# A third landing buffer for the feed-forward weight stream of a diffusion layer, in memory taken from two small tiles

## The chip, the cores and the metric

The kernel runs on one core of a Trainium2 chip. The metric is the device time of one execution in microseconds, and lower is better. The engines are named as the profile names them: PE is the matrix engine (PEld is its weight load), DVE the vector engine, ACT the scalar engine, POOL the GpSimd engine, SP the engine that issues most of the DMAs.

## The reference

One layer of a hybrid backbone on 128 context tokens and 256 latent tokens (384 in all, width 2048, float32). The parts that matter here:

```python
def layer(x, cond, s0_f, s0_b, n_chunks, lw):
    mod = jax.nn.silu(cond) @ lw['w_ada'] + lw['b_ada']
    sh1, sc1, ga1, sh2, sc2, ga2 = [m[:, None, :] for m in jnp.split(mod, N_MOD, axis=-1)]
    h = rmsnorm(x, lw['norm_pre_mix']) * (1.0 + sc1) + sh1
    m, s_f, s_b = mixer(h, s0_f, s0_b, n_chunks, lw)
    x = x + ga1 * rmsnorm(m, lw['norm_post_mix'])
    h = rmsnorm(x, lw['norm_pre_ffn']) * (1.0 + sc2) + sh2
    ff = (jax.nn.silu(h @ lw['w_ffn_gate']) * (h @ lw['w_ffn_up'])) @ lw['w_ffn_down']
    x = x + ga2 * rmsnorm(ff, lw['norm_post_ffn'])
    return x, s_f, s_b
```

`mixer` is a gated linear attention and a Fourier branch, whose inside the change does not touch. The feed-forward has 5632 hidden channels: gate and up weights of 2048 x 5632, down weights of 5632 x 2048. `cond` has two columns, one for context and one for latent tokens, and `mod` has six parts of 2048 channels each.

## The kernel before

**Stages.** The program runs in one pass: the first norm with the first two modulation parts and the first products (to 146 us in the profile below), the other input projections beside the attention, the Fourier branch and the merge (to about 740 us), the output projection (to 893 us), the second norm, and from about 910 us the feed-forward to the end. Weights come from memory in blocks of 128 x 1024 floats (512 KB).

**A weight block's way.** Each float32 matmul is done as three products of rounded parts. A block lands in a tile called `raw` (or `u`, `dw`, see below), ACT casts it to `whi` (lines 225 and 1431), DVE subtracts to get the remainder `wlo` (lines 226 and 1442), and PE takes both. `whi` and `wlo` have four buffers each, `raw` has two in the pool `wp`. The instructions of PE, ACT, DVE and POOL stand in the order in which the code records them; only those of SP are placed by a scheduler, and SP runs them in that order.

**The feed-forward.** The hidden width is cut into 11 chunks. Each chunk computes gate and up products in the steps A, B, C, E, F, G, H (`pgu`, with sums of blocks that save products, Strassen's way), and the down products of the chunk before are set between these steps (`pds`, `pdn`). Five kinds of step read a streamed block through `raw` (`STREAM`: C, G, D, DC, DG); the steps A, B, DA, DB read blocks that are kept in ten resident slots (`u`, `dw`) over several steps. Before each step, `grab2` takes the split block, issues further loads (`load_more`, line 1396) and splits the next one (`split_next`, line 1421). `load_more` keeps at most two streamed blocks loaded and not yet split (`out_now[0] < 2`), then up to two resident loads. Since there are two `raw` buffers, the load of a block waits on SP for the remainder of the block two before it (DVE, line 1442).

**Other work in the feed-forward.** DVE makes the sixth modulation part from small blocks `w<-in_w_ada` (line 1470 loads, line 1475 multiplies and adds; `ada_last`). Finished down products are added up in memory (`sums_d`): ACT copies them out, POOL issues an adding DMA (line 1667), and SP loads them back in the last chunk (`back` and `psums`, lines 1677 and 1693). Hidden blocks are turned by DMA from ACT's queue (line 1610), two per chunk, and ACT takes the result at line 1616 before it copies the sums of step A out (line 1574).

**The two small tiles.** `spad` holds silu of the conditioning, padded from 2 to 32 columns (2 KB a partition); PE reads it in the first stage as a stationary operand, and DVE reads its two real columns for parts three to six, to the end of the kernel. `adev` (1 KB a partition) takes the modulation sums `pr` out of PSUM before PE turns them (lines 585 and 1490). In the output projection the tile of the modulation sums `adacc` serves as two more landing buffers (`raw2`, line 1106).

Of the kernel before, what the change touches and what calls it, by code (L numbers as in the profile page):

```python
# [11 lines left out]
F32 = mybir.dt.float32  # L12
# [4 lines left out]
ALU = mybir.AluOpType  # L17
# [4 lines left out]
P = 128  # L22
D = 2048
KT = D // P
# [13 lines left out]
G = 1024  # L38
# [59 lines left out]
def tile_step(ctx: ExitStack, tc: tile.TileContext, a, o):  # L98
    nc = tc.nc
    PE, ACT, DVE, POOL, SP = nc.tensor, nc.scalar, nc.vector, nc.gpsimd, nc.sync  # L100
    ctx.enter_context(nc.allow_non_contiguous_dma(reason="small column loads"))

    const = ctx.enter_context(tc.tile_pool(name="const", bufs=1))
    actp = ctx.enter_context(tc.tile_pool(name="actp", bufs=1))
    wp = ctx.enter_context(tc.tile_pool(name="wp", bufs=4))
    dram = ctx.enter_context(tc.tile_pool(name="dram", bufs=1, space=DRAM))

    cond = const.tile([P, KT, 2], F32, name="cond")
    SP.dma_start(cond, a["cond"])
    spad = const.tile([P, KT, 32], F32, name="spad")  # L110
    POOL.memset(spad, 0.0)
    eps_t = const.tile([P, 1], F32, name="eps_t")
    ones = const.tile([P, P], F32, name="ones")
    POOL.memset(eps_t, EPS)
# [42 lines left out]
    for i in range(8):  # L157
        k = (0, 1, 1, 2, 1, 2, 1, 2)[i]
# [136 lines left out]
                    start=n == 0, stop=n == len(src) - 1,  # L295
                )

    def warm(dst, n):

        for _ in range(n):  # L300
            PE.matmul(dst, ones, spad.rearrange("p a b -> p (a b)")[:, 0:T], start=True, stop=True)
# [15 lines left out]
    pss = ctx.enter_context(tc.tile_pool(name="pss", bufs=5, space=PSUM))  # L317
    with ExitStack() as s:
        pa = s.enter_context(tc.tile_pool(name="pa", bufs=1))
        pb = s.enter_context(tc.tile_pool(name="pb", bufs=2))  # L320
        slabs = {}

# [53 lines left out]
        px = pss.tile([P, T], F32, tag="side", name="px")  # L376
# [51 lines left out]
            return mm, lambda dst=None: flush(lracc, kb == 0, dst)  # L428

        ACT.activation(spad[:, :, 0:2], cond, AF.Silu)  # L430
        ACT.activation(tmp1, eps_t, AF.Sqrt)
        qs = [pa.tile([P, T], F32, name=f"qsA{n}") for n in range(2)]
        for k in range(KT):
            sq = qs[k] if k < 2 else scr[:, 4 + k % 4, :]
            ACT.activation(sq, xn(k), AF.Square)
            if k >= 2:
                DVE.tensor_add(qs[k % 2], qs[k % 2], sq)
        warm(px, 11)

        for t in range(3):  # L440
            for n, q in enumerate(qs):
# [10 lines left out]
        ev = pb.tile([P, 256], F32, tag="ev", name="ev")  # L452
# [6 lines left out]
        for kb in range(KT):  # L459
# [31 lines left out]
            if kb:  # L491
                ev = pb.tile([P, 256], F32, tag="ev", name="ev")
# [10 lines left out]
            if kb == 0:  # L503
# [6 lines left out]
                op0=ALU.add, op1=ALU.mult,  # L510
            )
            DVE.tensor_scalar_add(mods[:, 0, kb, :], pm[:, 0:2], cols[:, 0, kb : kb + 1])
            for lo, hi, c in segs:
                DVE.tensor_scalar(
                    hf[:, lo:hi], xr[:, lo:hi], mods[:, 1, kb, c : c + 1], mods[:, 0, kb, c : c + 1],
                    op0=ALU.mult, op1=ALU.add,
# [43 lines left out]
    adap = ctx.enter_context(tc.tile_pool(name="adap", bufs=1))  # L560

    def ada_rest(todo):
        for m in todo:
            for half in range(2):
                acc = adap.tile([P, 2, 1024], F32, tag="adacc", name="adacc")
                for k in range(KT):
                    w = adap.tile([P, 1024], F32, tag="adaw", name="adaw", bufs=2)
                    SP.dma_start(w, a["w_ada"][m - 2, half, k])
                    for c in range(2):
                        if k == 0:  # L570
                            DVE.tensor_scalar_mul(acc[:, c, :], w, spad[:, k, c : c + 1])
                        else:
                            DVE.scalar_tensor_tensor(  # L573
                                acc[:, c, :], w, spad[:, k, c : c + 1], acc[:, c, :], op0=ALU.mult, op1=ALU.add,
                            )
                    yield
                yield
                pr = pss.tile([P, 256], F32, tag="side", name="pr")
                for c in range(2):
                    for j in range(4):  # L580
                        PE.matmul(
                            pr[32 * j : 32 * j + 32, :], selr[:, 32 * c : 32 * c + 32],
                            acc[:, c, j * 256 : (j + 1) * 256], start=c == 0, stop=c == 1,
                        )
                ev = adap.tile([P, 256], F32, tag="adev", name="adev")
                ACT.copy(ev, pr)
                yield
                pt = pss.tile([P, 2, P], F32, tag="side", name="ptm")
                for b in range(2):
                    PE.transpose(pt[:, b, :], ev[:, b * P : (b + 1) * P], ident)  # L590

                src = pt.rearrange("p b (j r) -> p j b r", r=32)
                mh = mods[:, m, 8 * half : 8 * half + 8, :]
                for c in range(2):
                    DVE.tensor_copy(mh[:, :, c].rearrange("p (j b) -> p j b", b=2), src[:, :, :, c])
                bc = lambda v: v[:, 8 * half : 8 * half + 8].unsqueeze(2).to_broadcast([P, 8, 2])
                DVE.tensor_add(mh, mh, bc(bsc1[:, 1, :] if m == 4 else cols[:, m, :]))
                w1 = {2: 1, 4: 2, 5: 3}.get(m)
                if w1 is not None:
                    DVE.tensor_mul(mh, mh, bc(norms[:, w1, :]))  # L600
# [12 lines left out]
    with ExitStack() as s:  # L613
# [203 lines left out]
        for c in range(2):  # L817

            dst = a2.rearrange("p (h d j) -> p d h j", d=2, j=P)[:, c]
            raw, up = (x.rearrange("p (h j) -> p h j", j=P) for x in (raw3[1 + c][0:98, 0:512], part[0:98]))  # L820
# [28 lines left out]
    with ExitStack() as s:  # L849
# [11 lines left out]
        pairs = [x[:, n * pw : n * pw + 2 * HT] for x, k in ((cl, 6), (d2, 2)) for n in range(k)]  # L861
# [184 lines left out]
    with ExitStack() as s:  # L1046
# [49 lines left out]
        for i in range(KT):  # L1096
            p = psm.tile([P, T], F32, tag="mm", name="pmm")
            for g in range(2):
                n = 2 * i + g - 2 * KT
                if n < -6:  # L1100
                    w = grab()
                else:

                    w = take()
# [162 lines left out]
        pf = s.enter_context(tc.tile_pool(name="pf", bufs=1))  # L1267
# [103 lines left out]
        pairs = []  # L1371
# [3 lines left out]
        for kind, c, i in steps:  # L1375
            e = [kind, c, i, None]
# [4 lines left out]
        for c in range(1, NFC):  # L1381
            resident += [(kind, c, i) for kind in "AB" for i in range(4)]
            if c < LAST:
                resident += [("DA", c - 1, 0), ("DB", c - 1, 0)]
        out_now = [sum(e[3] is not None for e in entries)]
        free = set(range(10))

        def slot(x, kind, c, i):
# [5 lines left out]
            return t.rearrange("p (i x) -> p i x", i=2 if kind[0] == "D" else FC)  # L1394

        def load_more(kept=1):
            while pairs and out_now[0] < 2:
                e, src = pairs.pop(0)
                e[3] = wp.tile([P, G], F32, tag="raw", name="raw", bufs=2)
                SP.dma_start(e[3] if e[0] == "R" else fold_of(e[0], e[3]), src)  # L1400
                out_now[0] += 1
            while kept and resident:
                kind, c, i = resident[0]
                k = slot(kind[-1] == "B", kind, c, i)
                if k not in free or k >= len(slots):
                    return
                free.remove(k)
                SP.dma_start(fold_of(kind, slots[k]), src_of(kind, c, i))
                resident.pop(0)
                kept -= 1  # L1410
# [53 lines left out]
        def ada_last():  # L1464
            m = 5
            acc, wt = (adap.tile([P, 2, 512], F32, tag="adaw", name=n, bufs=2) for n in ("acc5", "w5"))
            for q in range(4):
                for k in range(KT):
                    w = wt[:, k % 2, :]
                    SP.dma_start(w, a["w_ada"][m - 2, q // 2, k, :, 512 * (q % 2) : 512 * (q % 2) + 512])  # L1470
                    for c in range(2):
                        if k == 0:
                            DVE.tensor_scalar_mul(acc[:, c, :], w, spad[:, k, c : c + 1])
                        else:
                            DVE.scalar_tensor_tensor(
                                acc[:, c, :], w, spad[:, k, c : c + 1], acc[:, c, :], op0=ALU.mult, op1=ALU.add,
                            )
                    turned[0] = k == KT - 1
                    yield
                while d_live[0]:  # L1480
                    yield
                prt = psm.tile([P, 2, P], F32, tag="mm", name="pr")
                pr, pt = prt[:, 0, :], prt[:, 1, :]
                for c in range(2):
                    for j in range(4):
                        PE.matmul(
                            pr[32 * j : 32 * j + 32, :], selr[:, 32 * c : 32 * c + 32], acc[:, c, j * P : (j + 1) * P],
                            start=c == 0, stop=c == 1,
                        )
                ev = adap.tile([P, 256], F32, tag="adev", name="adev")[:, 0:P]  # L1490
                ACT.copy(ev, pr)
                yield
                PE.transpose(pt, ev, ident)

                mh = mods[:, m, 4 * q : 4 * q + 4, :]
                DVE.tensor_copy(mh, pt.rearrange("p (j r) -> p j r", r=32)[:, :, 0:2])
                bc = lambda v: v[:, 4 * q : 4 * q + 4].unsqueeze(2).to_broadcast([P, 4, 2])
                DVE.tensor_add(mh, mh, bc(cols[:, m, :]))
                DVE.tensor_mul(mh, mh, bc(norms[:, 3, :]))
                turned[0] = False  # L1500
                yield
# [11 lines left out]
        for u in range(HEAD):  # L1513
            kind, c, j = ffn_order[u]
            dst_of[kind](hp[u], c, j)
        n = 0
# [195 lines left out]
        for kind, c, i in steps:  # L1712
# [14 lines left out]
            if kind == "D":  # L1727
                w = grab2()
                n, kh = i // 2, i % 2
                if kh == 0:  # L1730
# [3 lines left out]
                    pool, tag = (pss, "side") if done % 2 or (c, n) == (NFC - 2, 3) else (psm, "mm")  # L1734
# [32 lines left out]
            elif kind[0] == "D":  # L1767
                w = grab2()
# [241 lines left out]
```

## Time and profile before

| | us |
|---|---|
| median of 3 runs | 1953.98 |
| lowest and highest run | 1950.4, 1955.69 |
| the profiled execution, its own time | 1949.2 |
| its span, first to last instruction | 1947.4 |
| PE busy in the span | 1926.3 |
| DVE, ACT busy | 1639.7, 1049.6 |

The span is what the profile covers; the execution's own time has 1.8 us more around it. The profiled execution is 4.8 us below the median and 1.2 us below the lowest of the timed runs. A row of the timeline gives the start, the duration, engine, line, operation and tiles, and in brackets the idle time before it with what ended it. A row of the waits gives who waited for whom: total in us, times, longest. A row of the windows gives for each stretch its length and each engine's busy time with the number of instructions.

### The profile page before, as it was taken

To read this page: it belongs to the slowest core of one execution; us is meant where nothing else is said; L and a number is where in the kernel's file an instruction comes from. 1 tells how busy PE (TensorE), PEld (TensorE's weight loads), DVE (VectorE), ACT (ScalarE), POOL (GpSimd) and SP (SyncE) were. 2 spreads that over 40 slices of the span, in tenths; PEclk is the share of its full clock that TensorE was granted. 3 is DMA by queue.
4 is the path that set the end of the run, shared out by engine and by line. 5 is a ranking of instruction groups with operands and counts; after the bars stand their busy time and mean duration, and the time that the engine had idled before them with its cause. 6 is when DMAs were issued, how large, how long until landed. Compare 5 with 4: busy or idle time off the path is not lost.

```text
span 1947.4 us, 27999 instructions
## 1 busy us (share of the span) xinstructions
PE 1926.3 (99%) x10434; PEld 1704.9 (88%) x10434; DVE 1639.7 (84%) x2059; ACT 1049.6 (54%) x1513; POOL 145.2 (7%) x171
## 2 busy tenths in 40 slices
PE   8999999999999999999999999999999999999998
PEld 5779999999999999999988888788888888888886
DVE  5569788879876788978798999899999999998876
ACT  4233454554336655447456665656565666666545
POOL 0000000000000000004000111111111120211001
PEclk9999999999999999999999999999999999999999
DMA  9977677667754687655539596968788787969554
GB/s 390 372 261 262 226 254 231 231 224 257 253 187 156 214 271 256 213 173 183 172 125 275 140 260 157 244 169 241 192 215 225 195 232 184 243 143 252 151 200 136
DMA packets 236649, 426.78 MB, mean 219 GB/s; under 512 B 35804, under 2 KB 140444, under 8 KB 232160
## 3 DMA queue, kind: packets, MB, share of 16 engines
q1 hardware_dynamic: 199072, 386.70, 59.6%
q0 software_dynamic: 18432, 33.56, 11.2%
q10 hardware_dynamic: 19008, 4.72, 1.6%
q8 instruction: 82, 1.34, 0.3%
q14 instruction: 55, 0.45, 0.1%
HBM read 365.68 MB, written 54.53 MB: 216 GB/s over the span
## 4 chain that ended last, share of the span: by engine, by line
PE 84%; DMA 5%; issue 4%; DVE 4%; ACT 2%; POOL 0%; SPq 0%; ACTq 0%; DVEq 0%; POOLq 0%
PE pmm L259 35%; PE pgu L1533 23%; PE pdn L1533 8%; PE pds L1533 5%; PE pv L399 3%; PE pgm L382 1%; DMA raw<-in_w_u 1%; DVE wlo L1442 1%; DMA slab<-in_w_ada 1%; PE pf L997 1%; PE px L417 1%; PE pmm L1252 1%; DMA ep<-ep 1%; ACT whi L1431 1%; PE bk L1533 1%
## 5 line engine op out<-in xcount | busy, mean ns | idle before, releaser
L259 PE MATMUL pmm<-A_hi,whi 128*128 128x384 f32 x1200 | 404.3, 337 | 0.0
L259 PE MATMUL pmm<-A_hi,wlo 128*128 128x384 f32 x1200 | 401.4, 334 | 0.0
L259 PE MATMUL pmm<-A_lo,whi 128*128 128x384 f32 x1200 | 401.3, 334 | 0.0
L225 ACT CAST whi<-raw 128x1024 fp32r<-128x1024 f32 x181 | 189.8, 1051 | 187.9 <-DMA raw<-in_w_gate 63.3
L1431 ACT CAST whi<-u 128x1024 fp32r<-128x1024 f32 x200 | 207.7, 1052 | 123.5 <-DVE u L1438 39.2
L226 DVE TENSOR_TENSOR wlo<-raw,whi 128x1024 fp32r<-128x1024 f32 x179 | 218.2, 1221 | 54.7 <-ACT whi L225 53.8
L1431 ACT CAST whi<-raw 128x1024 fp32r<-128x1024 f32 x157 | 165.4, 1053 | 174.3 <-DMA raw<-in_w_d 48.0
L1442 DVE TENSOR_TENSOR wlo<-u,whi 128x1024 fp32r<-128x1024 f32 x200 | 242.5, 1220 | 17.5 <-ACT whi L1431 17.4
L1533 PE MATMUL pgu<-whi,A_hi 128*128 128x512 f32 x640 | 251.6, 393 | 4.3 <-ACT ep L1574 3.1
L1533 PE MATMUL pgu<-whi,A_lo 128*128 128x512 f32 x640 | 249.4, 390 | 0.0
L259 PEld LDWEIGHTS pmm<-A_hi,whi 128*128 128x128 f32 x1200 | 225.3, 188 | 2.9 <-issue 1.8
L573 DVE SCALAR_TENSOR_TENSOR adacc<-adaw,spad,adacc 128x1024 f32<-128x1024 f32 x180 | 222.8, 1279 | 3.3 <-DMA adaw<-in_w_ada 2.9
L259 PEld LDWEIGHTS pmm<-A_lo,whi 128*128 128x128 f32 x1200 | 225.4, 188 | 0.2
L259 PEld LDWEIGHTS pmm<-A_hi,wlo 128*128 128x128 f32 x1200 | 225.2, 188 | 0.0
L1442 DVE TENSOR_TENSOR wlo<-raw,whi 128x1024 fp32r<-128x1024 f32 x157 | 191.6, 1221 | 15.9 <-ACT whi L1431 15.7
L1533 PE MATMUL pgu<-wlo,A_hi 128*128 128x512 f32 x640 | 185.9, 389 | 0.2 <-DVE wlo L1442 0.2
L1533 PEld LDWEIGHTS pgu<-whi,A_hi 128*128 128x128 f32 x640 | 120.1, 188 | 33.2 <-ACT ep L1574 4.0
L1533 PEld LDWEIGHTS pgu<-wlo,A_hi 128*128 128x128 f32 x640 | 120.1, 188 | 25.9 <-DVE wlo L1442 0.6
L1533 PEld LDWEIGHTS pgu<-whi,A_lo 128*128 128x128 f32 x640 | 120.2, 188 | 24.2
L1533 PE MATMUL pgu<-whi,S 128*128 128x512 f32 x400 | 116.7, 389 | 0.0
L1667 POOL DMA_DIRECT2D sums_d<-dw x64 | 58.6, 950 | 640.6 <-ACT dw L1663 366.3
L1533 PE MATMUL pdn<-whi,hid_hi 128*128 128x512 f32 x264 | 102.9, 390 | 0.0
(407 smaller groups left out, 3294.0 us busy)
## 6 DMA issues: line engine op xcount, KB each, us to landing
adaw<-in_w_ada SPq DMA_DIRECT2D x96, 512.0 KB, 4.1
raw<-in_w_d SPq DMA_DIRECT2D x70, 512.0 KB, 5.0
slab<-in_w_ada SPq DMA_DIRECT2D x32, 1024.0 KB
raw<-in_w_gate SPq DMA_DIRECT2D x64, 512.0 KB, 4.7
raw<-in_w_g SPq DMA_DIRECT2D x48, 512.0 KB, 3.9
raw<-in_w_u SPq DMA_DIRECT2D x48, 512.0 KB, 4.7
raw<-in_w_in SPq DMA_DIRECT2D x44, 512.0 KB, 4.3
u<-in_w_u SPq DMA_DIRECT2D x40, 512.0 KB, 7.0
```

The lines of the kernel that those rows point to most:

```text
L225: ACT.copy(hi, raw)
L226: sub = lambda: eng.tensor_sub(lo, raw, hi.bitcast(F32))
L259: PE.matmul(dst, w[wi][:, k * n + n0 : k * n + n0 + P], x[xi][:, k0 + k, :], start=first and k == 0 and j == 0, stop=last and k == kts - 1 ...
L382: PE.matmul(pgv[q : q + 32, :], spad[:, k, :], slab[k // (KT // 2)][:, k % (KT // 2), :], start=k < 4, stop=k >= KT - 4,)
L399: PE.matmul(pv[2 * t + g], hT[x_][:, kb, t * P : (t + 1) * P], w_[:, g * 512 : (g + 1) * 512], start=kb == 0 and j == 0, stop=kb == KT - 1 ...
L417: PE.matmul(px, w_[:, u * P : (u + 1) * P], hT[x_][:, kb, :], start=j == 0, stop=j == 2)
L573: DVE.scalar_tensor_tensor(acc[:, c, :], w, spad[:, k, c : c + 1], acc[:, c, :], op0=ALU.mult, op1=ALU.add,)
L997: PE.matmul(pf[:, 0 : 2 * HT], w[0][:, c], x[k], start=k == 0, stop=False)
L1431: ACT.copy(hi, src)
L1442: DVE.tensor_sub(lo, src, hi.bitcast(F32))
L1533: PE.matmul(dst, stat[x_][m], mov(w[w_], m), start=first and w_ == m == x_ == 0, stop=last and w_ == m == 1, skip_group_check=any(more),)
L1667: POOL.dma_start(sums_d[k], u, accum_op=ALU.add)
```

## The change

The conditioning tile `spad` moves into the pool `pa` of the first stage, whose memory is given back after it. DVE copies its two real columns over `cond`, which stays, and the later modulation reads `cond`. The tile `adev` goes: the sums are copied from PSUM into the first columns of the sum tile itself (`acc`), which PE has read by then. The memory buys one more `raw` tile in the pool `pf`, which opens after the output projection. `load_more` now keeps up to three streamed blocks, and each third of them lands in the new tile, so that a buffer comes round after three blocks.

```diff
-    spad = const.tile([P, KT, 32], F32, name="spad")
-    POOL.memset(spad, 0.0)
...
         pa = s.enter_context(tc.tile_pool(name="pa", bufs=1))
+        spad = pa.tile([P, KT, 32], F32, name="spad")
+        POOL.memset(spad, 0.0)
...
         ACT.activation(spad[:, :, 0:2], cond, AF.Silu)
+        DVE.tensor_copy(cond, spad[:, :, 0:2])
...
-                            DVE.tensor_scalar_mul(acc[:, c, :], w, spad[:, k, c : c + 1])
+                            DVE.tensor_scalar_mul(acc[:, c, :], w, cond[:, k, c : c + 1])
...
-                ev = adap.tile([P, 256], F32, tag="adev", name="adev")
+                ev = acc[:, 0, 0:256]
                 ACT.copy(ev, pr)
...
         out_now = [sum(e[3] is not None for e in entries)]
+        n_raw = [0]
...
-            while pairs and out_now[0] < 2:
+            while pairs and out_now[0] < 3:
                 e, src = pairs.pop(0)
-                e[3] = wp.tile([P, G], F32, tag="raw", name="raw", bufs=2)
+                n_raw[0] += 1
+                if n_raw[0] % 3:
+                    e[3] = wp.tile([P, G], F32, tag="raw", name="raw", bufs=2)
+                else:
+                    e[3] = pf.tile([P, G], F32, tag="raw", name="raw")
...
-                ev = adap.tile([P, 256], F32, tag="adev", name="adev")[:, 0:P]
+                ev = acc[:, 0, 0:P]
```

On PE and ACT the instructions keep their order, on DVE one copy is added near the start, and on POOL one memset moves. SP's queue is placed anew. Two places show it, with SP's rows in their order; `raw` are streamed blocks, `u` and `dw` resident ones, `w` the small modulation blocks, `back` the sums that come back, and the shape is that of the tile.

The first is the end of a middle chunk, where the down blocks and the next chunk's resident gate blocks are loaded. Before:

```order
L1400 DMA raw<-in_w_d 128x2x512
L1408 DMA dw<-in_w_d 128x2x512
L1408 DMA u_9222<-in_w_g 128x4x256
L1400 DMA raw<-in_w_d 128x2x512
L1470 DMA w_9748<-in_w_ada 128x512
L1408 DMA u_9222<-in_w_g 128x4x256
L1408 DMA u_9223<-in_w_g 128x4x256
L1470 DMA w_9748<-in_w_ada 128x512
L1400 DMA raw<-in_w_g 128x4x256
```

Now:

```order
L1406 DMA raw<-in_w_d 128x2x512
L1414 DMA dw<-in_w_d 128x2x512
L1414 DMA u_9217<-in_w_g 128x4x256
L1406 DMA raw<-in_w_g 128x4x256
L1476 DMA w_9745<-in_w_ada 128x512
L1414 DMA u_9217<-in_w_g 128x4x256
L1414 DMA u_9218<-in_w_g 128x4x256
L1476 DMA w_9745<-in_w_ada 128x512
L1406 DMA raw<-in_w_d 128x2x512
```

The places of the streamed loads among the others are the same, and each holds the block that stood one place later.

The second is the last chunk, where the sums come back. Before:

```order
L1400 DMA raw<-in_w_u 128x4x256
L1408 DMA u_9221<-in_w_u 128x4x256
L1400 DMA raw<-in_w_d 128x2x512
L1408 DMA u_9221<-in_w_u 128x4x256
L1677 DMA back<-sums_d 128x512
L1400 DMA raw<-in_w_u 128x4x256
L1400 DMA raw<-in_w_d 128x2x512
```

Now:

```order
L1406 DMA raw<-in_w_d 128x2x512
L1414 DMA u_9216<-in_w_u 128x4x256
L1406 DMA raw<-in_w_u 128x4x256
L1414 DMA u_9216<-in_w_u 128x4x256
L1683 DMA back<-sums_d 128x512
L1406 DMA raw<-in_w_d 128x2x512 x2
```

The last streamed up block stood behind the third load of sums and now stands ahead of it.

More of the change, by code (lines that the diff above doesn't have):

```diff
@@ L296, in tok_sum, with warm @@
                 )
-    def warm(dst, n):
+    def warm(dst, spad, n):
         for _ in range(n):
@@ L437, in tile_step @@
                 DVE.tensor_add(qs[k % 2], qs[k % 2], sq)
-        warm(px, 11)
+        warm(px, spad, 11)
         for t in range(3):
@@ L570, in ada_rest @@
                         if k == 0:
-                            DVE.tensor_scalar_mul(acc[:, c, :], w, spad[:, k, c : c + 1])
+                            DVE.tensor_scalar_mul(acc[:, c, :], w, cond[:, k, c : c + 1])
                         else:
                             DVE.scalar_tensor_tensor(
-                                acc[:, c, :], w, spad[:, k, c : c + 1], acc[:, c, :], op0=ALU.mult, op1=ALU.add,
+                                acc[:, c, :], w, cond[:, k, c : c + 1], acc[:, c, :], op0=ALU.mult, op1=ALU.add,
                             )
@@ L1472, in ada_last @@
                         if k == 0:
-                            DVE.tensor_scalar_mul(acc[:, c, :], w, spad[:, k, c : c + 1])
+                            DVE.tensor_scalar_mul(acc[:, c, :], w, cond[:, k, c : c + 1])
                         else:
                             DVE.scalar_tensor_tensor(
-                                acc[:, c, :], w, spad[:, k, c : c + 1], acc[:, c, :], op0=ALU.mult, op1=ALU.add,
+                                acc[:, c, :], w, cond[:, k, c : c + 1], acc[:, c, :], op0=ALU.mult, op1=ALU.add,
                             )
```

## The prediction

> **What bounds the kernel now.** I read the page's head first, then the windows, to see where PE, the busiest engine, is not busy.
>
> ```profile
> span 1947.4 us, 27999 instructions
> PE 1926.3 (99%) x10434; PEld 1704.9 (88%) x10434; DVE 1639.7 (84%) x2059; ACT 1049.6 (54%) x1513; POOL 145.2 (7%) x171
> ```
>
> The windows cut the feed-forward at the borders of its chunks. After the length come the busy time of PE, PEld, DVE, ACT and POOL, then PE's granted clock and the DMA engines' share.
>
> ```profile
> 910.00:1053.00 143.00, 143.00 (x711) 128.51 (x711) 124.32 (x144) 81.96 (x111) 12.05 (x10) 1.00 0.59 198
> 1053.00:1150.00 97.00, 95.07 (x416) 76.86 (x415) 88.73 (x93) 58.43 (x72) 11.54 (x13) 1.00 0.76 198
> 1150.00:1242.00 92.00, 92.00 (x422) 75.56 (x421) 86.40 (x93) 58.44 (x72) 14.03 (x16) 1.00 0.80 215
> 1242.00:1334.00 92.00, 89.67 (x396) 73.45 (x395) 84.58 (x88) 57.10 (x70) 14.04 (x16) 1.00 0.81 198
> 1334.00:1702.00 368.00, 368.00 (x1657) 303.43 (x1656) 347.06 (x366) 234.34 (x286) 56.16 (x64) 1.00 0.83 212
> 1702.00:1800.00 98.00, 96.97 (x442) 79.41 (x442) 84.34 (x86) 61.53 (x75) 14.03 (x16) 1.00 0.81 196
> 1800.00:1920.00 120.00, 119.99 (x537) 98.92 (x536) 96.19 (x104) 61.98 (x78) 2.65 (x3) 1.00 0.57 175
> ```
>
> PE is idle 1.93 + 2.33 + 1.03 + 0.01 = 5.30 us in the 1010 us from 910 to 1920, the whole stretch in which the new buffer is in use. Four chunks in a row, from 1334 to 1702, have no idle time at all. The last 27 us hold no streamed load. So whatever a better supply of weights does for this execution, it cannot give more than 5.30 us.
>
> The waits, asked of ACT, DVE and SP from 910 to 1920, show how the streamed blocks are supplied (who waited for whom: us, times, longest).
>
> ```profile
> ACT whi L1431 <- DMA raw<-in_w_d: 48.0, 16, 6.5
> ACT whi L1431 <- DMA raw<-in_w_g: 26.6, 13, 3.9
> ACT whi L1431 <- DMA raw<-in_w_u: 21.9, 9, 6.3
> DVE u L1441 <- DMA raw<-in_w_u: 19.4, 11, 5.2
> SPq L1400 <- DVE wlo L1442: 551.0, 151, 16.4
> ```
>
> A streamed load leaves as soon as a buffer is free: SP stood 551 us before such loads, 151 times, for the remainder (line 1442) that frees one. ACT stood 96.5 us for blocks that had not landed (48.0 + 26.6 + 21.9). But PE was idle only 5.3 us, because the four `whi` and `wlo` pairs are a stock between ACT and PE.
>
> The waits of PE in the same stretch name what ended its idle time:
>
> ```profile
> PE pgu L1533 <- ACT ep L1574: 3.1, 2, 2.2
> PE pgu L1533 <- ACT whi L1431: 1.0, 1, 1.0
> PE ptr L1597 <- DVE ep L1590: 0.6, 1, 0.6
> PE pgu L1533 <- DVE wlo L1442: 0.2, 1, 0.2
> ```
>
> Each has its own history, so I followed the holes back one at a time.
>
> **The hole that a streamed block makes.** In the last chunk, from the timelines of SP, ACT and PE:
>
> ```profile
> 1779.60 0.34 SPq L1677 DMA_DIRECT2D back<-sums_d  x1
> 1780.04 0.37 SPq L1400 DMA_DIRECT2D raw<-in_w_u  x1
> 1785.85 1.04 ACT L1431 CAST whi<-raw 128x1024 fp32r<-128x1024 f32 x1 [6.27 <-DMA raw<-in_w_u]
> 1786.95 0.50 PE L1533 MATMUL pgu<-whi,A_hi 128*128 128x512 f32 x1 [1.03 <-ACT whi L1431]
> ```
>
> The load stood behind the returning sums, landed 5.8 us after its issue, and ACT (6.27 us) and then PE (1.03 us) waited for it. In the new order it is ahead of these sums, one block's time earlier. That hole closes: 1.03 us.
>
> A second wait of ACT, the longest of all, shows what the change does in an ordinary chunk:
>
> ```profile
> 1117.54 0.37 SPq L1400 DMA_DIRECT2D raw<-in_w_u  x1
> 1124.60 0.37 SPq L1400 DMA_DIRECT2D raw<-in_w_d  x1
> 1131.57 1.05 ACT L1431 CAST whi<-raw 128x1024 fp32r<-128x1024 f32 x1 [6.49 <-DMA raw<-in_w_d]
> ```
>
> With three buffers the down block takes the place of the load before it and leaves near 1117.5. With the same 7.0 us to the cast (1131.57 - 1124.60) it is there at 1124.5, when ACT began to wait (1131.57 - 6.49 = 1125.1). So the 6.5 us on ACT go, but PE had only a sliver of idle time here.
>
> **The holes with another cause.** The largest, at a chunk border, follows a turning DMA (the first row is from the chain of waits, the others are ACT's and PE's):
>
> ```profile
> 1245.27 15.31 DMA ep<-ep
> 1260.60 1.33 ACT L1616 COPY ep<-ep 128x1024 uint16<-128x1024 uint16 x1 [2.90 <-DMA ep<-ep]
> 1262.70 1.42 PE pgu L1533 x5
> ```
>
> It ended 15.3 us after ACT put it out; ACT waited 2.90 us, copied the sums of step A late, and PE lost 2.21 of its 2.33 idle us in that window (the `L1574` row above has it as its longest, 2.2). The third cause is a modulation block:
>
> ```profile
> 1062.14 1.42 DVE L1475 SCALAR_TENSOR_TENSOR acc<-w,spad,acc 128x512 f32<-128x512 f32 x2 [4.38 <-DMA w<-in_w_ada]
> ```
>
> DVE stood 4.38 us, and the holes in the window from 1053 to 1150 come behind it: the 0.6 and the 0.2 us of the table, and the other `L1574` one, 3.1 - 2.2 = 0.9. Together 1.7 of 1.93 us. Neither the turning DMAs nor the modulation blocks get a buffer, and SP's new order leaves them where they were, behind as many loads. I cost both at nothing gained.
>
> What is left, 1.93 - 1.7 and 2.33 - 2.21, is 0.2 and 0.1 us, which I give to streamed blocks (the first lies just behind the ACT wait of 6.49). Gain in this execution: 1.03 + 0.3 = 1.3 us.
>
> **The other edits.** In the first microseconds:
>
> ```profile
> 0.74 0.53 POOL L111 MEMSET spad<- 128x512 f32 x1 [0.29 <-POOLq L1992]
> 1.66 0.29 POOL masks.py:199 TENSOR_SCALAR_AFFINE_SELECT ident<-ident 128x128 f32<-128x128 f32 x1
> 2.43 1.28 ACT L430 ACT_TABLE_LOAD   x1 [2.43 <-DMA cond<-in_cond]
> 3.73 0.23 ACT L430 ACTIVATE spad<-cond 128x32 f32<-128x32 f32 x1
> ```
>
> The memset moves behind the making of `ident`, to about 1.95 - 0.46 + 0.53 = 2.0 us; silu needs it at 3.73, after the load of `cond` and a table, which hide it. If they did not, it would cost up to 0.5 us. DVE's new copy of 32 columns lies near 4 us, ahead of sums whose inputs ACT makes afterwards; ACT's row of the same size took 0.23 us, so it is worth 0 to 0.2, and I take 0. The reads from `cond` in place of `spad` have the same shape.
>
> Copying the modulation sums into their own tile makes the output projection's extra landing buffer wait for the transposes too:
>
> ```profile
> 855.43 8.60 SPq L197 DMA_DIRECT2D raw<-in_w_out  x4
> 863.73 0.38 PE L590 MATMUL ptm<-ident,adev 128*128 128x128 f32 x2
> 872.33 1.05 ACT L225 CAST whi<-raw 128x1024 fp32r<-128x1024 f32 x1 [1.37 <-PE pmm L259]
> ```
>
> The first of those four loads went out at 855.43 into `raw2`. It now has to come after 864.1 (863.73 + 0.38), and SP's order puts it last of the four, at 855.43 + 8.60 = 864.0: 8.7 us later. Its block is cast just before the row at 872.33, at which ACT has 1.37 us to spare because PE still holds the buffers. With 5.8 us to landing, the longest above that I rest on, it is there by 870. Cost nothing, and 0 to 2 us if three loads at once land later.
>
> **From the profiled execution to the median.** It took 1949.2 us, the median is 1953.98: an ordinary run has 4.8 us more of something the trace cannot show. The clock was full in all these windows and the program is the same, so I take it to be late data. Between none and all of it can be streamed blocks; waits for DMA being mixed as above, I take half, 2.4 us. Sum: 1953.98 - 1.3 - 2.4 = **1950.3 us**; its own range is 1947.9 (all of the 4.8) to 1952.7 (none).
>
> The Trainium skill speaks to this in "Perfetto Trace Analysis", section "Identifying Performance Opportunities": a gap that repeats on the engine that should be saturated can mean that SBUF is too small for the next tile. Here the repeating gap is on ACT (38 waits), and PE's few holes have three causes; by that rule a buffer on this engine would bring little, which the sum says as well, where ACT's 96.5 us would promise far more.
>
> **The rivals.** *All late data goes.* ACT and DVE run ahead of PE, and so also take up late turning DMAs and modulation blocks. For: DVE's 19.4 us of waits for streamed blocks vanish, and it is 92% busy in a chunk (347.06 of 368), so its lateness is passed on. Against: the turning DMA's 15.3 us do not depend on it. Time: 1953.98 - 5.3 - 4.8 = 1943.9 at best, 1944 to 1948 in all. Chance 0.28.
>
> *Nothing on PE.* PE's stock already covers the loads, the holes come from the other causes and move about: 1953 to 1956, taken at 1954. It is also the case that three loads wait in a row for the same DMA engines, so that each just lands later. Chance 0.16.
>
> *The turning DMAs come late (slower).* Now up to three streamed loads lie in flight when a chunk's two turning DMAs go out from ACT's queue, with the DMA engines 0.81 busy. For: one of them took 15.3 us already, and PE lost 2.2 us when ACT waited 2.9, so from about 0.7 us of such a wait PE pays. Against: the new order has no more loads ahead of the border than before. If four more borders lose 2.2 us each, the time is 1953.98 - 1.3 + 8.8 = 1961.5. Chance 0.14. In "DMA: Bandwidth & Descriptors", section "Issuing engines are not separate DMA queues", the Trainium skill says that DMAs of all issuing engines run on the same 16 DMA engines and interleave; that is the ground for this rival, and no row here shows the share that each gets.
>
> **How the numbers follow.** The forecast has 0.42. About 0.3% (5.9 us) can be told from no change here, since the three runs differ by 5.3 us. Faster than 1948.1 is the second case (0.28) and the low end of the forecast (0.06): 0.34. Slower than 1959.8 is the last rival: 0.14. The rest, 0.52, lies within. The range goes from 1944, the best case, to 1957, over the case of nothing and into the last rival; it leaves out most of that rival and little else.
>
> **What would show it.** Right: ACT's three rows of waits for `raw` fall from 96.5 us to under 20, SP still waits for line 1442, the hole near 1787 is gone, the border holes of 1 to 2 us behind line 1574 remain, and the window from 1334 to 1702 takes as long as before. Wrong: waits at line 1616 at several borders, idle PE between 855 and 900, or ACT's waits for `raw` unchanged.

## The result, and the profile after

The changed kernel takes 1941.84 us (median of 6 runs, 1940.43 to 1943.04), against 1952.12 us (6 runs, 1950.03 to 1955.69) for the kernel before. The ratio is 0.9946, 95% interval 0.9933 to 0.9959: 10.3 us faster by the medians. The forecast of 1950.3 us was wrong, and the time lies 2.2 us below its range. The profiled execution took 1940.43 us, 8.8 us less than the profiled one of before (1949.2).

The head of the page:

```profile
span 1938.6 us, 28021 instructions
PE 1922.4 (99%) x10434; PEld 1705.8 (88%) x10434; DVE 1640.1 (85%) x2060; ACT 1056.3 (54%) x1513; POOL 144.9 (7%) x171
```

The span fell by 8.8 us (1947.4 to 1938.6). Only 4.9 us of that was idle time of PE; the other 3.9 us went from its *busy* time, 1926.3 to 1922.4, with the same 10434 matmuls. This is the first thing that the prediction did not have.

The chain of waits that ended last, by engine (before: PE 84%, DMA 5%, issue 4%, DVE 4%):

```profile
PE 96%; DMA 1%; DVE 1%; ACT 1%; issue 0%; SPq 0%; POOL 0%; DVEq 0%; ACTq 0%; POOLq 0%
```

The windows of the feed-forward, cut as before (length, then busy time and count of PE, PEld, DVE, ACT, POOL, then PE's clock, the DMA share and GB/s):

```profile
1053.00:1150.00 97.00, 96.98 (x429) 79.80 (x428) 90.39 (x94) 61.22 (x75) 11.51 (x13) 1.00 0.81 211
1242.00:1334.00 92.00, 92.00 (x410) 76.16 (x408) 87.34 (x91) 59.36 (x72) 14.00 (x16) 1.00 0.84 210
1334.00:1702.00 368.00, 368.00 (x1658) 304.00 (x1657) 348.53 (x366) 237.16 (x287) 56.02 (x64) 1.00 0.82 212
1702.00:1800.00 98.00, 98.00 (x449) 80.77 (x448) 83.65 (x83) 64.71 (x80) 16.64 (x19) 1.00 0.79 197
```

PE has no idle time left: 1.93, 2.33 and 1.03 us have become 0.02, 0 and 0. The counts show more than the busy times: from 1242 to 1334 PE now does 410 matmuls where it did 396, and from 1053 to 1150 it does 429 where it did 416. PE has no wait from 910 to 1910 in the view of waits.

Who still waits (us in total, times, longest), for ACT and SP in the feed-forward:

```profile
ACT whi L1437 <- PE pgu L1539: 101.0, 121, 2.5
ACT whi L1437 <- DMA raw<-in_w_u: 5.4, 3, 2.3
ACT whi L1437 <- DMA raw<-in_w_d: 4.2, 3, 2.3
ACT whi L1437 <- DMA raw<-in_w_g: 1.8, 2, 1.2
SPq L1406 <- DVE wlo L1448: 547.6, 149, 18.2
```

ACT's waits for `raw` fell from 96.5 to 11.4 us, as forecast. It now waits for PE instead: it is as far ahead as the four `whi` allow.

To see where the 8.8 us came from I laid the k-th matmul of one trace beside the k-th of the other. At 1064 the changed kernel is 0.2 us ahead, at 1895 it is 8.7 us ahead, and the lead grows at these places of before: 2.2 us from 1064 to 1076, 0.8 from 1132 to 1142, 2.5 at 1262, 0.5 from 1324 to 1329, 0.3 from 1601 to 1702, 1.3 at 1787, 0.5 at 1894. These are the holes of before, the turning DMA's and the modulation block's included. One execution stands for each kernel here, and the holes of two buffers are not the same in each: the one at 1262 has 2.21 us of idle time before, 1.69 in the run with two buffers below, and 0.22 in the kernel before with short pauses of DVE, and neither of these two runs has the one at 1787.

The hole at 1262 was the turning DMA's. ACT and PE at the same border now:

```profile
1239.61 1.89 ACTq L1616 DMA_TRANSPOSE ep<-ep  x1
1253.09 1.35 ACT L1622 COPY ep<-ep 128x1024 uint16<-128x1024 uint16 x1
1256.93 0.39 PE L1539 MATMUL pgu<-whi,A_hi 128*128 128x512 f32 x1
```

The second turning DMA goes out at 1239.61 (before: 1245.27), 17.3 us ahead of the matmul that needs what follows from it; before, that matmul started at 1262.70 after 2.21 us idle, so it could have started at 1260.5, 15.2 us after the issue. ACT no longer waits for the DMA (before: 2.90 us). The transfer did not get a buffer; it got a start some 2 us earlier in PE's time, because ACT reached the instruction that issues it earlier. It was also shorter this time, at most 13.5 us, as ACT took its result at 1253.09 without a wait. But with 15.31 us it would have landed at 1254.9 and held PE up by about 0.1 us only (an estimate: from there to PE it took 2.10 us before, 1260.60 to 1262.70).

The modulation block near 1062 shows the same on DVE:

```profile
1059.66 1.42 DVE L1481 SCALAR_TENSOR_TENSOR acc<-w,cond,acc 128x512 f32<-128x512 f32 x2 [4.38 <-DMA w<-in_w_ada]
```

DVE waits the same 4.38 us as before. But it does so 2.5 us earlier (1059.66 against 1062.14) while PE up to there is only 0.2 us earlier, and PE sees nothing of it. The block's load itself leaves SP earlier, at 1054.60 against 1057.36: in SP's queue it stands behind loads that wait for DVE's remainders, and DVE is earlier.

### The profile page after: what moved, and what is told of

It reads as the page before. It is cut to its first block, busy times and chain, and to the rows that moved or that the text cites. A ratio compares the mean times of both kernels' runs of the same rounds, so it can differ in the third digit from the quotient of the medians.

```text
span 1938.6 us, 28021 instructions
## 1 busy us (share of the span) xinstructions
PE 1922.4 (99%) x10434; PEld 1705.8 (88%) x10434; DVE 1640.1 (85%) x2060; ACT 1056.3 (54%) x1513; POOL 144.9 (7%) x171
## 3 DMA queue, kind: packets, MB, share of 16 engines
q0 software_dynamic: 18432, 33.56, 11.4%
## 4 chain that ended last, share of the span: by engine, by line
PE 96%; DMA 1%; DVE 1%; ACT 1%; issue 0%; SPq 0%; POOL 0%; DVEq 0%; ACTq 0%; POOLq 0%
PE pmm L257 35%; PE pgu L1539 31%; PE pdn L1539 10%; PE pds L1539 7%; PE pv L399 3%; PE pgm L382 1%; DMA slab<-in_w_ada 1%; PE pf L998 1%; PE px L417 1%; PE pmm L1253 1%; PE bk L1539 1%; PE po L647 1%; PE pf L999 0%; DMA raw<-in_w_br_gla 0%; PE pr L582 0%; PE dl L647 0%
## 5 line engine op out<-in xcount | busy, mean ns | idle before, releaser
L1437 ACT CAST whi<-u 128x1024 fp32r<-128x1024 f32 x200 | 209.1, 1053 | 168.7 <-PE pds L1539 48.4
L574 DVE SCALAR_TENSOR_TENSOR adacc<-adaw,cond,adacc 128x1024 f32<-128x1024 f32 x180 | 222.9, 1280 | 2.7 <-DMA adaw<-in_w_ada 2.2
L1539 PE MATMUL pdn<-whi,hid_lo 128*128 128x512 f32 x264 | 102.8, 390 | 0.0
```

The lines of the kernel that those rows point to most:

```text
L574: DVE.scalar_tensor_tensor(acc[:, c, :], w, cond[:, k, c : c + 1], acc[:, c, :], op0=ALU.mult, op1=ALU.add,)
L1437: ACT.copy(hi, src)
L1539: PE.matmul(dst, stat[x_][m], mov(w[w_], m), start=first and w_ == m == x_ == 0, stop=last and w_ == m == 1, skip_group_check=any(more),)
```

## The experiments

Three theories stood. **Stock**: with a third buffer ACT and DVE get further ahead of PE, and this lead hides whatever comes late. **Landing**: the new order on SP makes modulation blocks and turned halves land sooner. **Memory**: the freed memory and the new start gave part of it.

**Two buffers, all other edits kept.**

```diff
-            while pairs and out_now[0] < 3:
+            while pairs and out_now[0] < 2:
...
-                if n_raw[0] % 3:
-                    e[3] = wp.tile([P, G], F32, tag="raw", name="raw", bufs=2)
-                else:
-                    e[3] = pf.tile([P, G], F32, tag="raw", name="raw")
+                if True:
+                    e[3] = wp.tile([P, G], F32, tag="raw", name="raw", bufs=2)
```

> The changed kernel with two buffers and two loads in flight, as before; only the memory edits and the start stay. If the third buffer made the gain: as the kernel before, 1950 to 1954 us. If the memory edits had a part in it: below 1948.

Measured: 1948.55 us, the kernel before on that chip 1949.61; ratio 0.9997 (0.9984 to 1.0009). Its waits are those of before:

```profile
PE pgu L1537 <- ACT ep L1578: 3.1, 3, 1.7
ACT whi L1435 <- DMA raw<-in_w_d: 49.4, 16, 6.5
```

The memory edits are worth nothing that can be measured.

**Three buffers, with `load_more` keeping two loads as before.**

```diff
-            while pairs and out_now[0] < 3:
+            while pairs and out_now[0] < 2:
```

> Three buffers in turn, but SP's program keeps the order of the kernel before (two loads in flight when the program is written). The stock theory (ACT and DVE get further ahead of PE, and the stock of split blocks covers whatever comes late): a load goes out when its buffer is free, the order hardly matters, 1940 to 1944 us. The landing theory (the new order on SP makes the modulation blocks and the turning DMAs land sooner): over 1947.

Measured: 1941.19 us, ratio 0.9955 (0.9942 to 0.9968), the whole gain, and 7.4 us below the run with two buffers on the same chip. Its ACT waits 3.5 us for `raw<-in_w_d` (49.4 in the run above). But the edit did not keep SP's order. In the last chunk the up block goes out ahead of the third load of sums, as in the changed kernel:

```profile
1765.31 0.37 SPq L1406 DMA_DIRECT2D raw<-in_w_u  x1
1773.03 0.34 SPq L1683 DMA_DIRECT2D back<-sums_d  x1
1773.47 0.89 SPq L1406 DMA_DIRECT2D raw<-in_w_d  x2
```

Of the 858 DMAs that SP issues, 854 stand at the place that they have in the changed kernel, and only 592 at that of the kernel before; in the run with two buffers all 858 stand as before. The scheduler placed the queue anew, and the new order came with the third buffer in this run too. So it shows that the number in `load_more` doesn't matter. It doesn't show that the order on SP plays no part, and it leaves the landing theory open; the pauses of DVE below decide more about that.

**A pause of ACT at each border, in both kernels.** The first copy that takes a turned half (line 1616, now 1622) is done three times instead of once.

```diff
-                        pend.append(together(g1, e2))
+                        pend.append(lambda: [together(g1, e2)() for _ in range(3)])
```

> The kernel before, with the first copy that takes a turned half done three times over at each of 8 borders: ACT is held up by 2 x 1.33 = 2.7 us there, about the wait that cost PE 2.2 us near 1262. Both theories: no reserve in this kernel, so some 2 us at most borders, 8 x 2 = 16 us, 1960 to 1970 us.

> The changed kernel with the same pause of 2.7 us on ACT at each of 8 borders. The stock theory: the reserve takes it up, within 2 us of the changed kernel, 1941 to 1944 us. The landing theory: there is no reserve, the pause costs as much as in the kernel before, some 16 us, over 1950.

There turned out to be 9 such borders. Measured: 1966.75 us in the kernel before (17.1 more than its 1949.61), 1947.54 us in the changed one (5.7 more than 1941.84; by the ratios to the kernel before, 0.9991 with 0.9980 to 1.0002 and 0.9946, it is 8.8 us; against the run with three buffers before it, on the same chip, 6.4). PE's waits, first of the kernel before, then of the changed one, with the pause:

```profile
PE pgu L1533 <- ACT ep L1574: 14.8, 9, 3.6
```

```profile
PE pgu L1539 <- ACT ep L1580: 4.0, 2, 3.0
```

The same lateness stops PE at all nine borders in one kernel and at two in the other: the first (1075, 2.98 us) and the last (1816, 1.04). So the lead is real, but not everywhere; "within 2 us" was wrong, since at the first border the changed kernel has no lead at all.

**The pause made twice as long, to size the lead.** Five copies instead of three.

> The changed kernel with the first copy of a turned half done five times over: ACT is held up by 4 x 1.33 = 5.3 us at each of 8 borders. A lead of about 2.5 us: what goes beyond it is lost, 8 x 2.7 = 21 us, 1960 to 1970 us. A reserve of a whole block (some 5 us): under 1950.

Measured: 1982.31 us, more than either theory gave. PE's waits, and two of the nine holes:

```profile
PE pgu L1539 <- ACT ep L1580: 26.6, 9, 5.5
...
1370.49 0.79 PE L1539 MATMUL pgu<-whi,A_hi 128*128 128x512 f32 x1 [2.57 <-ACT ep L1580]
1563.03 0.50 PE L1539 MATMUL pgu<-whi,A_hi 128*128 128x512 f32 x1 [2.57 <-ACT ep L1580]
```

At the seven middle borders the holes are 2.0 to 2.9 us of idle time for a pause of 5.3: a lead of 2.4 to 3.3 us. The first hole is 5.52 us, no lead, and the last 3.79. In the kernel before, with the pause of 2.7 us, the nine holes add up to 14.8 us; without the first (3.6) and the last (2.3) that is 1.3 us each, a lead of 1.4. So with the third buffer the lead at these borders is about twice as long. The profiled span is 43.5 us longer than the changed kernel's: 26.6 us of idle time, above the forecast 21, some 2.4 us that the idle time doesn't show (0.27 for each of nine holes, explained below; by this measure all these leads are 0.2 to 0.3 us shorter), 2.4 us already there before 910, and the rest, about 12 us, the slow clock behind holes, told at the end.

**One and two blocks fewer split ahead.** The lead itself is cut: once or twice, at the end of chunk 0, `grab2` takes a block without splitting another.

```diff
-        n_raw = [0]
+        n_raw, lead = [0], [True] * 20 + [False]
...
-            split_next()
+            split_next() if not lead or lead.pop(0) else None
```

> The changed kernel, still with three buffers, but one block is not split ahead: from the end of chunk 0 on, ACT and DVE are one block less in front of PE in program order. The stock theory: the reserve is this lead, so holes come back, 1944 to 1955 us. The landing theory (blocks and turned halves simply land sooner): as the changed kernel, 1940 to 1944.

> The same with two blocks fewer split ahead. The stock theory: with almost no lead left, holes at every border, over 1960 us. The landing theory: 1940 to 1944.

Measured: 1961.98 us with one block less, 1998.13 us with two. With one block less, three buffers notwithstanding, the old holes are back, and ACT again waits for turned halves:

```profile
PE pgu L1539 <- ACT ep L1580: 12.9, 7, 2.3
ACT ep L1622 <- DMA ep<-ep: 17.3, 7, 3.0
```

The loss was larger than the 2 to 13 us expected. With two blocks less, PE waits for remainders instead (38.6 us, 36 times), and not at the borders as expected. SP's order also differs here (777 and 707 of 858 DMAs stand as in the changed kernel), so these two show the direction rather than a size.

**A pause of DVE away from the borders.** The first multiplication of a modulation block is repeated at four places (near 993, 1180, 1368, 1552).

```diff
                         if k == 0:
-                            DVE.tensor_scalar_mul(acc[:, c, :], w, cond[:, k, c : c + 1])
+                            for _ in range(12 if c == 0 else 1):
+                                DVE.tensor_scalar_mul(acc[:, c, :], w, cond[:, k, c : c + 1])
```

> The kernel before, with the first multiplication of a modulation block done 12 times over at 4 places in the feed-forward (near 993, 1180, 1368 and 1552): DVE is held up by 11 x 0.39 = 4.3 us at each, as long as its wait of 4.38 near 1062. The stock theory: little lead here, 1 to 3 us at most of them, 4 to 12 us slower than before.

> The changed kernel with the same pauses of 4.3 us on DVE. The stock theory: taken up, 1940 to 1944 us. The landing theory: as many us lost as in the kernel before with these pauses.

Measured: 1963.63 us in the kernel before (13.1 more than 1950.49, just over the 4 to 12 expected), 1961.6 us in the changed kernel, 19.8 more than 1941.84. The stock theory's forecast for the changed kernel was plainly wrong: most of the pause is not taken up. The landing theory's was wrong too, since the changed kernel loses more than the kernel before; a spell of slow clock is part of that, and the rest stays open. Two rows of it, the pause on DVE and one hole it makes:

```profile
1182.28 6.62 DVE L1480 TENSOR_SCALAR acc<-w,cond 128x512 f32<-128x512 f32 x13
...
1213.30 0.73 PE L1540 MATMUL pds<-wlo,hid_hi 128*128 128x512 f32 x2 [1.20 <-DVE wlo L1448]
```

The pause is 6.62 - 0.88 = 5.7 us long, not 4.3 (0.88 us is what the two multiplications take without it), twice the lead found above. And DVE does not win it back: from 1182 to 1216 each of its rows starts where the one before ended, so 31 us later PE still pays. DVE is 93 to 95% busy in the changed kernel's windows from 1053 to 1702 (348.53 of 368; the prediction's 347.06 of 368 is 94%, not 92%), and a lead lost on it returns slowly. By matched matmuls PE loses 1.5 us to the third pause, at 1406, and more to the other three.

At the next border this pause brings the old hole back. ACT gets to the turning DMA late again, and PE loses 3.84 us of idle time:

```profile
1249.89 2.54 ACTq L1617 DMA_TRANSPOSE ep<-ep  x1
1266.65 1.33 ACT L1623 COPY ep<-ep 128x1024 uint16<-128x1024 uint16 x1 [3.54 <-DMA ep<-ep]
```

PE's matmul could have started at 1264.9, 15.0 us after the issue: the distance of before (15.2), and no longer 17.3. All three buffers are there, and SP's order from 1050 on is the changed kernel's to the last DMA. So a late DVE reopens this hole although the buffer and the order are there (the transfer was also longer, 16.7 us), and the landing theory, in which the order on SP closes it, does not fit.

That left a lead that hides about 2.5 us, or a DVE with no reserve. A shorter pause (5 repetitions in place of 12) tells them apart:

> The changed kernel with the four pauses on DVE cut to 4 x 0.39 = 1.6 us each. The theory as it now stands (the third buffer brings ACT and DVE about 2.5 us further ahead of PE at the places where the kernel before ran dry, and only lateness below that is hidden): taken up, 1941 to 1944 us. The rival (DVE is too busy to have any reserve, each pause goes through to PE): 4 x 1.6 = 6 us, 1947 to 1949.

> The kernel before with the same four pauses of 1.6 us on DVE. Both theories: no lead to spare at most of these places, 3 to 7 us slower than before.

Measured: 1943.63 us in the changed kernel, within the 1941 to 1944 expected, and 1949.04 in the kernel before, whose own median there was 1948.14 (ratios 0.9974, 0.9962 to 0.9985, and 1.0001, 0.9987 to 1.0014). By its ratio the first is 5.5 us behind the changed kernel's 0.9946, by its median 1.8; its trace decides. The pause is 2.1 us (2.97 for six multiplications, less 0.88). PE's only rows with a wait in this run of the changed kernel, from 910 to 1910:

```profile
1066.07 0.63 PE L1604 MATMUL ptr<-ident,ep 128*128 128x128 f32 x4 [0.61 <-DVE ep L1597]
1074.46 0.50 PE L1540 MATMUL pgu<-whi,A_hi 128*128 128x512 f32 x1 [0.91 <-ACT ep L1581]
```

These follow the first pause, at the first border, which has no lead. They are the holes of the modulation block, as long as before (0.63 and 0.93 us of idle time), and its row shows why they are back:

```profile
1061.64 1.42 DVE L1482 SCALAR_TENSOR_TENSOR acc<-w,cond,acc 128x512 f32<-128x512 f32 x2 [4.38 <-DMA w<-in_w_ada]
```

It comes 2.0 us later than in the changed kernel (1059.66), by about the length of the pause, while PE up to there is 0.1 us later; its load left at 1056.56, again 2.0 us later, from the same place in SP's order. After the other three pauses PE has no wait at all up to 1910. So DVE has a reserve of at least 2.1 us there and less than 5.7. The kernel before lost about 0.9 us, within what the comparison can tell, where 3 to 7 were expected: at most of these places it too had about 2 us to spare.

No version tried beats the changed kernel; the one whose `load_more` keeps two loads equals it. No run has the third buffer with the old order of SP, so the two stand for one change here.

## Why the prediction was wrong

**The bound of 5.30 us from PE's idle time: failed.** The gain in the feed-forward of the profiled execution was 8.5 us, where the sum had 1.3. Idle time under-counts holes, as matmuls overlap in the records. In the changed kernel, behind a row of narrow matmuls:

```profile
1250.00 0.48 PE L1539 MATMUL pgu<-whi,A_hi 128*128 128x512 f32 x1
1250.32 0.39 PE L1539 MATMUL pgu<-whi,A_lo 128*128 128x512 f32 x1
1250.55 0.40 PE L1539 MATMUL pgu<-whi,A_hi 128*128 128x512 f32 x1
```

A matmul of 512 columns is recorded as 0.39 us, yet the next starts 0.23 us after it. So a gap of 0.16 us between starts shows as no idle time, and the first wide matmul behind a break costs another 0.11 us (0.48 to 0.50 long, the next 0.32 to 0.34 later; at 1262 in the kernel before too). A hole is therefore about 0.27 us larger than its idle time: the one at 1262 was 2.21 us idle and 2.5 us long. By starts, the delays over 0.1 us from 910 to 1910 add up to 9.5 us before and 2.1 us after (a delay is what a start lies beyond the median spacing behind a matmul of that shape). The count of matmuls in a window, which the prediction quoted, would have told: 396 in 92 us against 1657 x 92 / 368 = 414 in a full chunk, though the kinds of matmul differ a little from one window to the next.

**"I cost both at nothing gained" (the turning DMA and the modulation block): failed, and this is the main step.** They gave 2.5 us and 2.2 us, over half of the gain. The step asked whether the transfer itself gets a buffer or a better place on SP. It does not. But the instruction that issues the turning DMA, and the one that waits for the modulation block, sit on ACT and DVE behind the casts and remainders of streamed blocks. As those stopped waiting (96.5 to 11.4 us), all that stands behind them came 2 to 2.5 us earlier in PE's time. The pauses of DVE put both back with all three buffers in place. This was the rival *All late data goes*, in its own words, and the time lies 2 us below the best that I gave it, since it was built on the same 5.3 us.

**The objection to that rival, that the turning DMA's 15.3 us do not depend on the buffer: beside the point.** The duration need not shrink; its start moves.

**The other streamed holes, put at 0.2 and 0.1 us: under-sized.** The places from 1132 to 1142 and from 1324 to 1329 gave 0.8 and 0.5 us.

**The hole near 1787: closed as forecast, under-sized.** 1.3 us against 1.03, by the rule above. The place in SP's order was not the whole cause: in the run with two buffers, in the same order, the load landed 4.3 us after its issue (5.8 before), ACT waited 3.94 us and PE not at all. The stretch from 1334 to 1702 passes as forecast: 0.3 us gained in 368.

**The other edits at nothing: right,** by the run with two buffers. The later load in the output projection cost nothing: the changed kernel is 0.2 us ahead at 740 and still so at 1064.

**Half of the 4.8 us surplus: not settled, and its size was wrong.** With six runs the surplus of median over profiled run is 2.9 us and not 4.8, and 1.4 after. Medians of the kernel before in later groups were 1949.61, 1950.49 and 1948.14 us, so a good part of the 4.8 us was the scatter of three runs. The spread is smaller too (5.7 us before, 2.6 after), which fits fewer holes, but no run isolates it.

**The slower rival: did not come.** ACT has no wait at the copies that take turned halves (4.3 us at line 1616 before), and the DMA engines' share is 0.79 to 0.84 in the windows shown (0.76 to 0.83 before).

The Trainium skill's rule on consistent bubbles, from "Perfetto Trace Analysis", section "Identifying Performance Opportunities", names a gap that repeats on the engine that should be saturated as a sign of too little SBUF. I read it as speaking against a large gain, because the repeating gap was on ACT. The runs differ from that reading: the 38 waits on the feeding engine went with one more buffer (96.5 us to 11.4), and it was worth 7 to 10 us.

## What to carry to other kernels

When an edit takes waits from an engine that feeds the bottleneck, price everything that stands behind those waits on that engine: the DMAs it issues and the other data it waits for all come earlier, and holes "of another cause" close with them. Measure holes of PE by the spacing of matmul starts, or by matmuls per window, not by idle time. A lead has a size (here 2.4 to 3.3 us at most borders, none at the first); lateness beyond it passes to PE. And when a scheduler places a queue, read the order that ran in the trace before an experiment on the order is believed.

## What the hardware showed that was not expected

After some holes PE's granted clock halves. In the kernel with the long pause, behind the two holes of 2.57 us quoted above (length, PE busy and count, clock, DMA share, GB/s):

```profile
1370.50:1373.50 3.00, 3.00 (x7) 0.50 0.06 8
1563.10:1566.10 3.00, 3.00 (x13) 1.00 0.11 13
```

Seven matmuls in 3 us against thirteen, behind holes of the same length. Over all the runs, in the feed-forward, no hole of up to 2.03 us of idle time had matmuls 0.43 us apart behind it, of the twelve from 2.04 to 2.57 six had, and all six from 2.86 us up had. The longest such spell, behind a hole of 2.86 us at 1272, put another 2.9 us between the matched matmuls of this kernel and the changed one. The Trainium skill, in "TensorE: Matmul & The Clock Gate", section "HAM oscillation — how this bites in real kernels", gives about 3.4 us as the idle gap from which this happens; here gaps of 2.04 us were enough at times. The kernel before, with 2.21 us at 1262, lies in the range in which it can happen; it did not there.
